# Operand sums of the second FFN product: on GpSimd, or in DRAM by copies and accumulating DMAs

## The chip, the core and the metric

The kernel runs on one core of a Trainium2 chip. The metric is the device time of one execution in microseconds (us). Matmuls run on TensorE (PE in the profile), the rest on VectorE (DVE), ScalarE (ACT) and GpSimd (POOL); SyncE (SP) issues most of the DMAs, POOL those that add to their destination.

## What is computed

One inference step of a two-layer encoder, for 1024 prompt rows and 64 sample rows (1088 in all) of width 1024, in float32. Layer 0 is a Mamba-2 mixer and a feed-forward block, layer 1 a band attention and a feed-forward block. The change concerns the feed-forward blocks:

```python
def swiglu(u, w_in, w_out):
    g, up = jnp.split(u @ w_in, 2, axis=-1)
    return (jax.nn.silu(g) * up) @ w_out

xp = xp + rmsnorm(swiglu(rmsnorm(xp, nw[2]), ffn_w_in[layer], ffn_w_out[layer]), nw[3])
```

`w_in` is 1024 x 5632, `w_out` 2816 x 1024. The output must agree with the float32 result, so each operand is split into a high and a low part and every product takes three matmuls.

## The kernel before, in words

**Layout.** Activations are kept transposed: features on the 128 partitions, rows of the batch on the free axis. The 1088 rows form four quarters of 256, 256, 288 and 288; half 0 (b = 0) is the two of 256, half 1 (b = 1) the two of 288.

**Two FFN products, both in a seven-product scheme.** Both large products are done by the Strassen-Winograd scheme: a matrix is cut into 2 x 2 quarters, and seven products of sums of quarters replace eight. The first FFN product (`run_pair`) does it for each pair of weight tiles: seven products P1 to P7 of 12 matmuls each, whose evictions by DVE, ACT and POOL give two hidden tiles. A few hidden tiles of half 0 are made by plain products (`plain_pairs`) instead. For the hidden matrix, the quarters are a11, a12, a21, a22: the row index is the quarter of the half, the column index the half of the 22 hidden tiles (`c, k = divmod(t_, K2)`, K2 = 11). The second FFN product needs, for each k of 0 to 10, the seven operands a11, a12, a22 and the sums s1, s2, s3, s4.

**Where the operands are kept.** `Hidden` keeps them in a DRAM scratch (`hscr`), one tensor for each layer and half, `[128, 7, 11 * n]` with n = 256 or 288; `OPS` gives the place of each operand. `Hidden.put` is called as each quarter of a (b, k) is done. It stores a11, a12 and a22 at once (SP, L1292) and keeps a21. When all four are there, POOL makes the sums in SBUF and each is stored by SP:

| line | sum | tile |
|---|---|---|
| L1307 | s3 = a11 - a21 | s3 |
| L1309 | s1 = a21 - a22 | in place of a21 |
| L1311 | s2 = s1 - a11 | in place of a11 |
| L1313 | s4 = a12 + s2 | in place of a12 |

The compiler moves instructions, so that L1307 (which needs only column 0) is seen after the first pair of a k, and the other three after the second.

**Order of the first product.** Six plain pairs of half 0 (k = 8 to 10, both columns), then 16 pairs of weights that serve both halves (k = 0 to 7; the middle), then six pairs for half 1 alone (k = 8 to 10; the tail). The weights of a pair come by two loads of 512 KB (SP, L253) into two raw buffers; POOL subtracts quarters (L291, L292), DVE adds (L309, L310), and ACT and DVE split the sums into high and low parts (L341, L342; for one quarter POOL does the low part, L342). The evictions are L1368 to L1388: L1371 is DVE's for P6, L1373 that for P2, and L1385 and L1388 are POOL's multiplications that end a hidden tile.

**Order of the second product.** `SEQ` lists the operands: a11, s2, s3, s1, a22, a12, s4, each for four output tiles p, 11 values of k and both halves (s4 one half after the other): 264 matmuls an operand. `loader` brings the operands from DRAM (SP, L1422) in this order, two values of k in a tile, and splits them (L1423, L1424). It takes an operand 9 us (`HD_W`) of planned time after its store. The products are added by DVE (ACT for the first) into the four quarters of the output (L1584 to L1597), which begin to leave in a22 and s4.

**Planned time.** The order of instructions is made by a planner (`Stream`): its clock `st.t` advances with the matmuls that are emitted (2360 columns a us), and side tasks are generators that run when their delay in it has passed. Matmuls keep their order as written; the other engines' instructions are ordered by priority and readiness when the program is built. Every engine takes its own queue in order, and so does SP with its DMAs: one that waits holds all behind it.

**The same kind of sum for the weights.** The sums of the second product's weights are made in DRAM already (`side_sums`, scratch `tscr`), during the mixers: copies by SP (L588), additions by accumulating DMAs from POOL (L591), each held until the newest matmul emitted at that point has run:

```python
def now(x):
    tc.add_manual_dep(x.ins, last[0].ins.name, AT, reason="its turn")
```

Of the kernel before, what the change touches and what calls it, by code (L numbers as in the profile page):

```python
# [16 lines left out]
P = 128  # L17
# [17 lines left out]
K2 = FT // 2  # L35
# [12 lines left out]
ES = 0.5, 0.5, 0.0  # L48
OS = 1.9, 1.4
EP_W, ER_W, EQ_W = (4.0, 7.0, 7.0, 5.0), (5.0, 8.9, 8.9, 7.0), 24.0  # L50
TS_W, HD_W, UT_W = 15.0, 9.0, 24.0

HIP = 3000
BYP = 0, 0, 800, 800
# [322 lines left out]
def hybrid_kernel(  # L377
# [197 lines left out]
    for b in range(2):  # L575
        for half in range(2):
            W.plan(*[dict(src=[w_so[m][:, half * 1024:(half + 1) * 1024]]) for mg in MGS for m in mg])

    def side_sums(layer):

        w2, td = w_f2[layer], td_[layer]
        KH = K2 * P

        def now(x):
            tc.add_manual_dep(x.ins, last[0].ins.name, AT, reason="its turn")

        def plain(p, i, src):
            now(nc.sync.dma_start(td[:, p, i], src))  # L588

        def more(p, i, src):  # L590
            now(G.dma_start(td[:, p, i], src, accum_op=ALU.add))  # L591
# [624 lines left out]
    def chain(layer, q, y, ss, cw, xsrc, xout, cpre, done):  # L1216
# [63 lines left out]
    class Hidden:  # L1280
# [9 lines left out]
        def write(self, op, b, k, x):  # L1290
            n = self.ops[b].n
            nc.sync.dma_start(self.hd[b][:, OPS[op], k * n:(k + 1) * n], x)  # L1292
            self.written[op, b, k] = st.t

        def put(self, t_, b, half, x):

            c, k = divmod(t_, K2)
            row = half ^ b
            got = self.got.setdefault((b, k), {})
            nm_ = f"a{row + 1}{c + 1}"  # L1300
            got[nm_] = x
            if nm_ != "a21":
                self.write(nm_, b, k, x)
            if len(got) == 4:
                g = G.tensor_tensor
                s3 = self.tmp.tile([P, 288], F32, tag=f"s3{b if k in BOTH else k % 2}", name="s3")[:, :self.ops[b].n]
                g(s3, got["a11"], got["a21"], op=ALU.subtract)  # L1307
                self.write("s3", b, k, s3)
                g(got["a21"], got["a21"], got["a22"], op=ALU.subtract)  # L1309
                self.write("s1", b, k, got["a21"])  # L1310
                g(got["a11"], got["a21"], got["a11"], op=ALU.subtract)  # L1311
                self.write("s2", b, k, got["a11"])
                g(got["a12"], got["a12"], got["a11"], op=ALU.add)  # L1313
                self.write("s4", b, k, got["a12"])

    def plain_pairs(ts, ops, hid, px):

        n = ops.n
        ws = [(W.get(), W.get()) for t_ in ts]
        for q in range(2):  # L1320
            st.wait_for(lambda: all(a_ in ops.plain for a_ in (f"a{q + 1}1", f"a{q + 1}2")))
            uq = ops.plain[f"a{q + 1}1"] + ops.plain[f"a{q + 1}2"]
            for t_, w2 in zip(ts, ws):
                x = hid.tile(t_, 0, q)

                def gate(ps):
                    with tc.high_priority(HIP):
                        A.activation(x, ps[:, :n], AF.Silu)

                def mult(ps):  # L1330
                    with tc.high_priority(HIP):
                        V.tensor_tensor(x, ps[:, :n], x, op=ALU.mult)
                    hid.put(t_, 0, q, x)

                for w, e in zip(w2, (gate, mult)):
                    unit(w, uq, n, e, pl=px)
                    if q:
                        W.put()

    def run_pair(t_, pr, bs, ends, ops, hid, px, tmp, apart=False):  # L1340


        tb = {b: {} for b in bs}
        for (p_, key, c0, i), b in [(x, b) for b in bs for x in PRODS] if apart else [(x, b) for x in PRODS for b in bs]:
            h, v = pr[key]
            n, x = ops[b].n, tb[b]

            def t_new(tag):
                return tmp.tile([P, n], F32, tag=f"{tag}{b if len(bs) > 1 else t_ // K2}", name=tag)

            st.wait_for(lambda: i in ops[b].hl)
            ah, al = ops[b].hl[i]
            ps = (px.tile([P, 512], F32, tag="mm", name="px") if p_ != P1 else mm("px"))[:, :n]
            for k in range(4):
                wh, wl = h[:, c0 + k * P:c0 + (k + 1) * P], v[:, c0 + k * P:c0 + (k + 1) * P]
                PE.matmul(ps, wh, ah[:, k, :], start=(k == 0), stop=False)  # L1356
                PE.matmul(ps, wh, al[:, k, :], start=False, stop=False)  # L1357
                last[0] = PE.matmul(ps, wl, ah[:, k, :], start=False, stop=(k == 3))  # L1358
                if k == 1:
                    st.run(6 * n / MMR)  # L1360
            st.t += 6 * n / MMR
            if b in ends:
                for r in ops[b].rings[i]:
                    r.put()
            with tc.high_priority(HIP):
                if p_ == P1:
                    x["p1"] = t_new("p1")
                    A.copy(x["p1"], ps)  # L1368
                elif p_ == P6:
                    x["u2"] = t_new("u2")  # L1370
                    V.tensor_tensor(x["u2"], ps, x["p1"], op=ALU.add)  # L1371
                elif p_ == P2:
                    V.tensor_tensor(x["p1"], ps, x["p1"], op=ALU.add)  # L1373
                    A.activation(x["p1"], x["p1"], AF.Silu)
                elif p_ == P7:
                    x["u3"] = hid.tile(t_, b, 1)
                    V.tensor_tensor(x["u3"], ps, x["u2"], op=ALU.add)
                elif p_ == P5:
                    x["c22"] = hid.tile(t_, b, 0)
                    V.tensor_tensor(x["c22"], ps, x["u3"], op=ALU.add)  # L1380
                    V.tensor_tensor(x["u2"], ps, x["u2"], op=ALU.add)
                elif p_ == P4:
                    V.tensor_tensor(x["u3"], ps, x["u3"], op=ALU.add)
                    A.activation(x["u3"], x["u3"], AF.Silu)
                    G.tensor_tensor(x["u3"], x["u3"], x["c22"], op=ALU.mult)  # L1385
                else:
                    V.tensor_tensor(x["u2"], ps, x["u2"], op=ALU.add)
                    G.tensor_tensor(x["c22"], x["p1"], x["u2"], op=ALU.mult)  # L1388
# [10 lines left out]
    def back(layer, start, cpost, xsrc, xmid, cpre, cpost2, xout, rb_out, done2):  # L1399

        dn, ops, phase, hid = [], [Ops(0, layer), Ops(1, layer)], [0], {}
        with ExitStack() as es:
# [152 lines left out]
            for op, bs in SEQ:  # L1555
# [3 lines left out]
                for p in range(4):  # L1559
# [17 lines left out]
                    for b in bs:  # L1577
# [3 lines left out]
                        c21, c22 = yq[q2][:, p, :], yq[q2][:, 4 + p, :]  # L1581
                        with tc.high_priority(HIP):
                            if op == "a11":
                                A.copy(c11, ps[b])  # L1584
                            elif op == "s2":
                                V.tensor_tensor(c12, ps[b], c11, op=ALU.add)
                            elif op == "a12":
                                V.tensor_tensor(c11, ps[b], c11, op=ALU.add)
                            elif op == "s3":
                                V.tensor_tensor(c21, ps[b], c12, op=ALU.add)  # L1590
                            elif op == "s1":
                                V.tensor_tensor(c22, ps[b], c21, op=ALU.subtract)
                                V.tensor_tensor(c12, ps[b], c12, op=ALU.subtract)
                            elif op == "a22":
                                V.tensor_tensor(c21, ps[b], c21, op=ALU.add)
# [537 lines left out]
```

## Time and profile before

| what | value |
|---|---|
| median of 3 runs (lowest, highest) | 3026.42 us (3023.85, 3032.41) |
| the profiled execution | 3029.47 us |
| its span, first to last instruction | 3027.8 us |
| mean granted TensorE clock | 0.985 of full |
| mean DMA rate | 131 GB/s |

The profile gives, for each engine, the time in which it executed something, for each group of instructions the count, the mean time and the idle time ahead of it with what ended it, and for each DMA the time from issue to landing. A DMA's issue has the line of its statement; waits of an issuing queue are marked SPq. Times in the views are counted from the start of the span. In a line of the timeline, the bracket has the idle time of the engine just before and who ended it. "issue" is time in which an engine waited for nothing that the profile shows.

### The profile page before, as it was taken

How to read it: one execution, taken by the hardware profiler on the slowest of the kernel's cores; microseconds unless marked ns; L12 is line 12 of the kernel's file. 1: busy time of each engine (PE TensorE's matmuls, PEld its weight loads, DVE VectorE, ACT ScalarE, POOL GpSimd, SP SyncE). 2: the span in 40 equal slices, each digit the busy share in tenths (PEclk: the TensorE clock that was granted, in tenths of full speed). 3: DMA queues.
4: the chain of work that ended last, by engine and by line, in shares of the span. 5: the costliest groups of instructions: out<-in, count | busy, mean ns of one | idle time of the engine just before them, and what ended most of it. 6: DMA issues, size and time to landing. Idle time of an engine off the chain costs nothing. (4 is left out here: it accounts for less than half of the span.)

```text
span 3027.8 us, 58411 instructions
## 1 busy us (share of the span) xinstructions
PE 2916.3 (96%) x22247; PEld 2850.9 (94%) x22247; DVE 2104.0 (69%) x4679; ACT 1447.8 (48%) x2677; POOL 903.7 (30%) x1081
## 2 busy tenths in 40 slices
PE   8999999999999999989998899999999999998998
PEld 7999999989999999989997899999899999998998
DVE  7778788885768554566569777777768754566457
ACT  6756565663453332234345556556554322333343
POOL 1333333340123545562023000000033555455011
PEclk9999999999999999999999999999999999999999
DMA  3023343345654223245565234444476232244565
GB/s 120 33 89 99 95 99 93 99 112 156 190 152 139 95 98 100 98 147 191 173 196 167 82 108 128 116 110 115 136 220 202 93 110 92 96 148 155 181 214 175
DMA packets 215273, 395.39 MB, mean 131 GB/s; under 512 B 21040, under 2 KB 138928, under 8 KB 214992
## 3 DMA queue, kind: packets, MB, share of 16 engines
q1 hardware_dynamic: 208592, 362.22, 36.6%
q0 software_dynamic: 6400, 29.43, 5.6%
q8 instruction: 175, 2.87, 0.4%
q14 instruction: 106, 0.87, 0.1%
HBM read 306.14 MB, written 127.12 MB: 143 GB/s over the span
## 5 line engine op out<-in xcount | busy, mean ns | idle before, releaser
L456 PE MATMUL mm<-r,hl 128*128 128x384 f32 (+2 forms) x1664 | 557.4, 335 | 7.2 <-DVE dt L738 3.4
L458 PE MATMUL mm<-r,hl 128*128 128x384 f32 (+2 forms) x1664 | 543.4, 327 | 4.9 <-DVE hl L355 4.2
L457 PE MATMUL mm<-r,hl 128*128 128x384 f32 (+2 forms) x1664 | 542.4, 326 | 0.0
L342 DVE TENSOR_TENSOR hl<-raw,hl 128x1024 fp32r<-128x1024 f32 (+2 forms) x219 | 250.4, 1144 | 155.3 <-ACT hl L341 154.6
L1357 PE MATMUL px<-r,hl 128*128 128x288 f32 (+1 forms) x1184 | 349.8, 295 | 0.0
L456 PEld LDWEIGHTS mm<-r,hl 128*128 128x128 f32 x1664 | 318.6, 191 | 9.6 <-ACT BT L815 3.7
L1356 PE MATMUL px<-r,hl 128*128 128x288 f32 x1056 | 314.2, 298 | 13.5 <-DVE u L1371 13.3
L458 PEld LDWEIGHTS mm<-r,hl 128*128 128x128 f32 x1664 | 318.0, 191 | 7.0 <-DVE hl L355 6.0
L457 PEld LDWEIGHTS mm<-r,hl 128*128 128x128 f32 x1664 | 318.7, 192 | 0.0
L1358 PE MATMUL px<-r,hl 128*128 128x288 f32 x1056 | 313.0, 296 | 0.0
L341 ACT CAST hl<-raw 128x1024 fp32r<-128x1024 f32 (+2 forms) x219 | 204.2, 938 | 201.1 <-PE po L1572 95.6
L482 POOL TENSOR_TENSOR ssum<-ssum,sq 128x256 f32<-128x256 f32 (+1 forms) x108 | 113.7, 1059 | 532.8 <-ACT sq L481 520.2
L1357 PEld LDWEIGHTS px<-r,hl 128*128 128x128 f32 x1184 | 224.8, 190 | 0.0
L1358 PE MATMUL px<-rx,hl 128*128 128x256 f32 x768 | 216.1, 281 | 6.7 <-DVE hl L342 6.7
L1356 PE MATMUL px<-rx,hl 128*128 128x256 f32 x768 | 216.5, 282 | 2.8 <-ACT hl L341 2.8
L1356 PEld LDWEIGHTS px<-r,hl 128*128 128x128 f32 x1056 | 200.6, 190 | 15.7 <-DVE u L1371 15.6
L1358 PEld LDWEIGHTS px<-r,hl 128*128 128x128 f32 x1056 | 200.4, 190 | 0.1
L1572 PE MATMUL po<-r,hl 128*128 128x288 f32 x616 | 182.8, 297 | 4.0 <-DVE hl L342 4.0
L1572 PE MATMUL po<-rx,hl 128*128 128x256 f32 x616 | 173.0, 281 | 12.7 <-DVE hl L342 12.7
L1570 PE MATMUL po<-r,hl 128*128 128x288 f32 x616 | 183.2, 297 | 0.0
L1571 PE MATMUL po<-r,hl 128*128 128x288 f32 x616 | 182.8, 297 | 0.0
L1357 PE MATMUL px<-rx,hl 128*128 128x256 f32 x640 | 179.7, 281 | 0.0
(365 smaller groups left out, 8547.3 us busy)
## 6 DMA issues: line engine op xcount, KB each, us to landing
raw<-in_w_f_dram SPq DMA_DIRECT2D x112, 512.0 KB, 3.4
tscr<-in_w_f_dram POOLq DMA_DIRECT2D x32, 704.0 KB, 7.0
raw<-in_w_in_dram SPq DMA_DIRECT2D x40, 512.0 KB, 3.4
r<-hscr SPq DMA_DIRECT2D x70, 288.0 KB, 4.8
hscr<-hid SPq DMA_DIRECT2D x132, 144.0 KB, 1.9
rx<-hscr SPq DMA_DIRECT2D x70, 256.0 KB, 3.7
hscr<-hid SPq DMA_DIRECT2D x132, 128.0 KB, 1.7
raw<-in_w_so_dram SPq DMA_DIRECT2D x32, 512.0 KB, 3.7
```

The source lines that it names most:

```text
L341: self.nc.scalar.copy(h, v)
L342: (eng or self.eng or self.nc.vector).tensor_tensor(lo, v, h, op=ALU.subtract)
L456: PE.matmul(ps[:, :n], h_, xh, start=(first and i == 0), stop=False)
L457: PE.matmul(ps[:, :n], h_, xl, start=False, stop=False)
L458: last[0] = PE.matmul(ps[:, :n], l_, xh, start=False, stop=(end and i == nk - 1))
L482: (eng or G).tensor_tensor(ssum[:, :n], ssum[:, :n], q[:, :n], op=ALU.add)
L1356: PE.matmul(ps, wh, ah[:, k, :], start=(k == 0), stop=False)
L1357: PE.matmul(ps, wh, al[:, k, :], start=False, stop=False)
L1358: last[0] = PE.matmul(ps, wl, ah[:, k, :], start=False, stop=(k == 3))
L1570: PE.matmul(ps[b], wh, xh, start=(k == 0), stop=False)
L1571: PE.matmul(ps[b], wh, xl, start=False, stop=False)
L1572: PE.matmul(ps[b], wl, xh, start=False, stop=(k == K2 - 1))
```

## The change

The operands of the second product are summed in DRAM.

- The quarters a11 and a22 (row and column equal) are kept with turned sign: in the plain pairs the multiplication, in the fast pairs the eviction ahead of it (P5's or P3's) is a scalar_tensor_tensor with the factor -1 in place of a tensor_tensor.
- `put` stores a11, a12 and a22 in their places and a21 by one DMA into both s3 and s1.
- When all quarters of a piece of k (0 to 3, 4 to 7, 8 to 10; `PCS`) are stored for a half, a task `sums` is spawned with a delay of `HD_W` = 9 us. It adds the turned a11 to s3 (which becomes a21 - a11) and the turned a22 to s1 by accumulating DMAs from POOL; 9 us (`SC_W`) later SP copies s1 to s2, 9 us later POOL adds the turned a11 to it, 9 us later SP copies s2 to s4, 9 us later POOL adds a12. Each is held by `now`, which moves out of `side_sums`.
- No POOL sums and no stores of sums are left.
- `OPS` is reordered (s3 beside s1), `SEQ` takes s3 ahead of s2, and the evictions of the second product follow the new order and signs: s2's product is added into two quarters, so there is one DVE instruction more for each p and half.

```diff
-TS_W, HD_W, UT_W = 15.0, 9.0, 24.0
+TS_W, HD_W, UT_W, SC_W = 15.0, 9.0, 24.0, 9.0
...
-    OPS = dict(a11=0, s2=1, a12=2, s3=3, s1=4, a22=5, s4=6)
+    OPS = dict(a11=0, a22=1, a12=2, s3=3, s1=4, s2=5, s4=6)
+    PCS = (range(0, 4), range(4, 8), range(8, 11))
 
     SEQ = (
-        ("a11", (0, 1)), ("s2", (0, 1)), ("s3", (0, 1)), ("s1", (0, 1)), ("a22", (0, 1)), ("a12", (0, 1)),
+        ("a11", (0, 1)), ("s3", (0, 1)), ("s2", (0, 1)), ("s1", (0, 1)), ("a22", (0, 1)), ("a12", (0, 1)),
...
         def put(self, t_, b, half, x):
 
             c, k = divmod(t_, K2)
-            row = half ^ b
-            got = self.got.setdefault((b, k), {})
-            nm_ = f"a{row + 1}{c + 1}"
-            got[nm_] = x
-            if nm_ != "a21":
-                self.write(nm_, b, k, x)
-            if len(got) == 4:
-                g = G.tensor_tensor
-                s3 = self.tmp.tile([P, 288], F32, tag=f"s3{b if k in BOTH else k % 2}", name="s3")[:, :self.ops[b].n]
-                g(s3, got["a11"], got["a21"], op=ALU.subtract)
-                self.write("s3", b, k, s3)
...
+            n = self.ops[b].n
+            nm_ = f"a{(half ^ b) + 1}{c + 1}"
+            cols = slice(k * n, (k + 1) * n)
+            if nm_ == "a21":
+                nc.sync.dma_start(self.hd[b][:, OPS["s3"]:OPS["s1"] + 1, cols], x.unsqueeze(1).to_broadcast([P, 2, n]))
+            else:
+                nc.sync.dma_start(self.hd[b][:, OPS[nm_], cols], x)
+                self.written[nm_, b, k] = st.t
+            got = self.got.setdefault((b, [k in r for r in PCS].index(True)), [])
+            got.append(k)
+            if len(got) == 4 * len(set(got)) and len(set(got)) == len(PCS[[k in r for r in PCS].index(True)]):
+                st.spawn(self.sums(b, min(got), max(got) + 1), HD_W)
+
+        def sums(self, b, k0, k1):
+
+            n, hd = self.ops[b].n, self.hd[b]
+            cols = slice(k0 * n, k1 * n)
+
+            def more(op, x):
+                now(G.dma_start(hd[:, OPS[op], cols], hd[:, OPS[x], cols], accum_op=ALU.add))
+                for k in range(k0, k1):
+                    self.written[op, b, k] = st.t
+
+            def copy(op, x):
+                now(nc.sync.dma_start(hd[:, OPS[op], cols], hd[:, OPS[x], cols]))
+
+            yield 0, 0
+            more("s3", "a11")
+            more("s1", "a22")
+            for op, x, y in (("s2", "s1", "a11"), ("s4", "s2", "a12")):
+                yield 0, SC_W
+                copy(op, x)
+                yield 0, SC_W
+                more(op, y)
...
-                        V.tensor_tensor(x, ps[:, :n], x, op=ALU.mult)
+                        if q == t_ // K2:
+                            V.scalar_tensor_tensor(x, ps[:, :n], -1.0, x, op0=ALU.mult, op1=ALU.mult)
+                        else:
+                            V.tensor_tensor(x, ps[:, :n], x, op=ALU.mult)
...
                     x["c22"] = hid.tile(t_, b, 0)
-                    V.tensor_tensor(x["c22"], ps, x["u3"], op=ALU.add)
+                    if 1 ^ b == t_ // K2:
+                        V.scalar_tensor_tensor(x["c22"], ps, -1.0, x["u3"], op0=ALU.mult, op1=ALU.subtract)
+                    else:
+                        V.tensor_tensor(x["c22"], ps, x["u3"], op=ALU.add)
...
-                    V.tensor_tensor(x["u2"], ps, x["u2"], op=ALU.add)
+                    if b == t_ // K2:
+                        V.scalar_tensor_tensor(x["u2"], ps, -1.0, x["u2"], op0=ALU.mult, op1=ALU.subtract)
+                    else:
+                        V.tensor_tensor(x["u2"], ps, x["u2"], op=ALU.add)
...
                             if op == "a11":
-                                A.copy(c11, ps[b])
+                                A.activation(c11, ps[b], AF.Copy, scale=-1.0)
+                            elif op == "s3":
+                                V.tensor_tensor(c21, c11, ps[b], op=ALU.subtract)
                             elif op == "s2":
                                 V.tensor_tensor(c12, ps[b], c11, op=ALU.add)
+                                V.tensor_tensor(c21, ps[b], c21, op=ALU.add)
```

More of the change, by code (lines that the diff above doesn't have):

```diff
@@ L577, in hybrid_kernel, with now @@
             W.plan(*[dict(src=[w_so[m][:, half * 1024:(half + 1) * 1024]]) for mg in MGS for m in mg])
+    def now(x):
+        tc.add_manual_dep(x.ins, last[0].ins.name, AT, reason="its turn")
     def side_sums(layer):
@@ L582, in side_sums @@
         KH = K2 * P
-        def now(x):
-            tc.add_manual_dep(x.ins, last[0].ins.name, AT, reason="its turn")
         def plain(p, i, src):
@@ L1288, in tile @@
             return self.tmp.tile([P, 288], F32, tag=f"{('c22', 'u3')[half]}{i}{t_ // K2}", name="hid")[:, :self.ops[b].n]
[L1290 to L1293, printed above, removed]
         def put(self, t_, b, half, x):
             c, k = divmod(t_, K2)
-            row = half ^ b
-            got = self.got.setdefault((b, k), {})
-            nm_ = f"a{row + 1}{c + 1}"
-            got[nm_] = x
-            if nm_ != "a21":
-                self.write(nm_, b, k, x)
-            if len(got) == 4:
-                g = G.tensor_tensor
-                s3 = self.tmp.tile([P, 288], F32, tag=f"s3{b if k in BOTH else k % 2}", name="s3")[:, :self.ops[b].n]
-                g(s3, got["a11"], got["a21"], op=ALU.subtract)
-                self.write("s3", b, k, s3)
[L1309 to L1314, printed above, removed]
@@ L1594, in back @@
                             elif op == "a22":
-                                V.tensor_tensor(c21, ps[b], c21, op=ALU.add)
+                                V.tensor_tensor(c21, c21, ps[b], op=ALU.subtract)
                             else:
```

2 lines of the change are left out of this document (removed).

## The prediction

> **What bounds the kernel now.** I read the page first, then the table of stages, then the chain of waits inside the stage that the change touches.
>
> ```profile
> span 3027.8 us, 58411 instructions
> PE 2916.3 (96%) x22247; PEld 2850.9 (94%) x22247; DVE 2104.0 (69%) x4679; ACT 1447.8 (48%) x2677; POOL 903.7 (30%) x1081
> ```
>
> TensorE is busy for 2916.3 of 3027.8 us, and the change leaves every matmul in place. So it can win at most what TensorE loses today near the code that it touches, and it loses whenever it makes TensorE wait. POOL's 30% says nothing by itself; what counts is whether a POOL instruction ends a wait of TensorE. I therefore looked for places where matmuls are missing. The table of stages gives, for five stretches, the matmuls done (x behind PE busy) and the granted clock (the third figure from the end).
>
> ```profile
> 1100.00:1300.00 200.00, 199.94 (x1604) 199.74 (x1604) 103.75 (x184) 61.44 (x103) 101.98 (x101) 1.00 0.33 109
> 1316.00:1387.00 71.00, 62.30 (x424) 61.04 (x425) 47.56 (x63) 25.11 (x39) 44.50 (x33) 0.93 0.42 135
> 2701.00:2783.00 82.00, 68.31 (x475) 66.92 (x473) 58.71 (x78) 33.13 (x51) 51.44 (x40) 0.93 0.44 144
> 940.00:975.00 35.00, 29.46 (x230) 28.86 (x229) 32.22 (x34) 14.28 (x18) 17.85 (x12) 0.90 0.34 109
> 2340.00:2368.00 28.00, 23.21 (x183) 22.81 (x182) 25.22 (x25) 11.53 (x15) 17.95 (x10) 0.94 0.32 105
> ```
>
> The first stretch is the middle of the first FFN product of layer 0, where every weight pair serves both token halves: TensorE never stops, and 200.00 us / 1604 = 0.1247 us for one matmul of 272 columns on average (256 and 288 take turns), so 0.132 us for one of 288. The next two are its tails in layers 0 and 1, in which six weight pairs serve only half 1 (288 columns). There 424 matmuls should take 56.0 us and took 71.0; 475 should take 62.7 and took 82.0. The last two are its heads, where the plain pairs give way to the first fast pair: at 0.1247 they should take 28.7 and 22.8 us and took 35.0 and 28.0. So a tail loses 15.0 us in layer 0 and 19.3 in layer 1, part of it at a granted clock of 0.93 after each stop, and a head loses 6.3 and 5.2. Of the 19.3, 4.2 are this row, the first matmul of the second product, which waits for the load of an operand that the change doesn't touch:
>
> ```profile
> PE po L1572 <- DVE hl L342: 4.2, 1, 4.2
> ```
>
> What stops TensorE in a tail is seen in the chain of waits of layer 1 (start, us, what):
>
> ```profile
> 2725.35 0.62 POOL tt L291
> ...
> 2726.62 0.83 POOL hid L1385
> 2727.45 1.67 POOL half L342
> 2729.12 1.69 POOL tt L292
> 2730.81 1.74 POOL hid L1388
> 2732.63 1.66 POOL hid L1309
> 2734.37 0.82 POOL hid L1311
> 2735.25 1.69 POOL hid L1313
> 2736.95 0.32 SPq L1292
> 2737.37 3.69 DMA raw<-in_w_f_dram
> 2741.19 1.33 POOL tt L291
> 2742.55 1.29 DVE tt L309
> 2743.89 1.52 issue
> 2745.41 0.46 DVE u L1371
> 2745.91 0.40 PE px L1356
> ```
>
> Read from the bottom: TensorE waits for DVE's eviction L1371, which stands in DVE's queue behind the weight sum L309, which waits for POOL's L291, which waits for the weights. Their load starts only at 2737.37, because SP takes its queue in order and the store ahead of it (L1292) waits for L1313. L1309, L1311 and L1313 are sums that the change removes, with L1307. The waits carry it: the largest of TensorE between 2695 and 2780 us is
>
> ```profile
> PE px L1356 <- DVE u L1371: 6.4, 3, 2.9
> ```
>
> **What the change removes.** Each of 11 hidden rows k, 2 halves and 2 layers loses four POOL sums (176 instructions). In a tail they come in turns: one after the first pair of a k (L1307), three after the second.
>
> ```profile
> 2718.51 1.67 POOL L1307 TENSOR_TENSOR s<-hid 128x288 f32<-128x288 f32 x1
> 953.38 4.20 POOL L1307 TENSOR_TENSOR s<-hid 128x256 f32<-128x256 f32 x1 [9.54 <-DVE hid L1332]
> 957.54 1.32 POOL L291 TENSOR_TENSOR tt<-raw 128x512 f32<-128x512 f32 x1
> ```
>
> In the chain the three sums lie between the end of L1388 and SP's store: from 2732.63 to 2736.95, 4.3 us. One L1307 is 1.67. L291 recurred after 15.8 us (2725.35 to 2741.19); 15.8 - 4.3 = 11.5, where TensorE needs 84 x 0.132 = 11.1 for a pair. After the edit the store after L1388 is the last thing ahead of the load, so what is late next is that load's own 3.69 us, and 0.4 us of each pair stay. Tail: 13 of the 15 us come back, **-13** in each layer (bounds -15, all of it, and -5, if the load is then held by its buffer and only L1307 counts, 3 x 1.67).
>
> In the head L1307 took 4.20 us and L291 followed at once. L291 could start as soon as its weights have landed, which the rows don't date, so between 0 and 4.2 us: **-3**, nearer to the upper end since L291 had no wait of its own left.
>
> **What it adds.** Each piece (rows 0 to 3, 4 to 7, 8 to 10) of each half gets four accumulating DMAs issued by POOL and two copies issued by SP, and the store of a21 becomes one of double size. A piece of four rows is 512 KB (half 0) or 576 KB (half 1). The nearest rows are those of the weight sums of the same form:
>
> ```profile
> q1 hardware_dynamic: 208592, 362.22, 36.6%
> q0 software_dynamic: 6400, 29.43, 5.6%
> tscr<-in_w_f_dram POOLq DMA_DIRECT2D x32, 704.0 KB, 7.0
> tscr<-tscr SPq DMA_DIRECT2D x16, 704.0 KB, 4.3
> hl<-in_w_f_dram POOLq DMA_DIRECT2D x7, 512.0 KB, 10.6
> L591 POOL DMA_DIRECT2D tscr<-in_w_f_dram x32 | 26.6, 831 | 225.5 <-PE mm L458 213.2 <-PE mmx L458 6.5 <-DVE zs L768 5.6
> SPq L588 <- PE mm L458: 78.3, 16, 13.0
> ```
>
> q0 spent 5.6% of 3027.8 = 170 us of all 16 engines on 29.43 MB, 5.76 us a MB: 3.0 us for 512 KB and 3.4 for 576 KB. The 704 KB (0.72 MB) is 4.15 by that and landed after 7.0, so 2.9 us are delay. q1 has 1108 us for 362.22 MB, 3.06 us a MB: a copy is 1.8 us. Both halves end a piece together, so four accumulating DMAs queue up: 2 x 3.0 + 2 x 3.4 + 2.9 = 15.7 us until s1 of half 1 has landed. The generator lets SP take the copy 9 us (SC_W) after those were issued. It waits for that landing, and SP takes nothing behind it: the stores L1292, the next weight loads L253, in the second product the operand loads L1422. So SP stands 15.7 - 9 = 6.7 us, once per piece. The second round has two accumulating DMAs, 3.0 + 3.4 + 2.9 = 9.3 us against 9, and holds nothing. On POOL each issue is 0.83 us (L591), against 0.8 to 1.7 for each sum removed; behind one that waits for its copy stand L291, L1385 and L1388 of the next pair; the copy is issued 9 us earlier and lands in 4.3, so an accumulating DMA of the second round waits only where SP's hold passed 4.7 us, by 2 us.
>
> Where does a hold of 6.7 us show? In the middle of the first product there is room:
>
> ```profile
> 1194.18 1.31 POOL L291 TENSOR_TENSOR tt<-raw 128x512 f32<-128x512 f32 x1 [6.18 <-DVE hid L1380]
> 1203.75 0.42 DVE L1371 TENSOR_TENSOR u<-px,p 128x256 f32<-128x256 f32 x1 [2.95 <-PE px L1358]
> ```
>
> From L291 to L1371 were 9.6 us here and 4.2 in the chain above (2741.19 to 2745.41), where nothing was spare: 5.4 us of cover. The loads there also come after the sums that go, some 4 us earlier, so 9.4 us cover 6.7 and the cost is nothing; without the cover it would be 6.7 and a stretch at half clock. In the tail the second piece ends just as the six pairs begin, and pairs then follow at 11.5 against 11.1: no cover but a start some 2 to 4 us earlier. I put it at **+7** in each layer: 6.7, less 2, and some 2 for the clock that falls after a stop (the stretches above were granted 0.93; bounds 0 if SP's copy falls behind the loads, +12 if the accumulating DMAs share the engines with the loads and land at 20 us).
>
> At the start of the second product the third piece follows with three rows; s3 is needed some 30 us later (the first operand is 264 matmuls at 0.1247 = 33 us) and s2 another 33 later, against 9 + 15.7 and 18 + 15.7 + 9.3 us: covered by the first operand. For SP's hold against the weights there, **+1** (0 to +4). The eight additional DVE evictions of that product in a layer and the turned sign cost TensorE nothing:
>
> ```profile
> L1586 DVE TENSOR_TENSOR yq<-po,yq x16: 418/437/458, 1436.5 to 2847.1; 128x256 f32<-128x256 f32 x8, 128x288 f32<-128x288 f32 x8
> L1477 DVE SCALAR_TENSOR_TENSOR yq<-yq,pcs,rb x56: 471/493/2657, 1577.0 to 3009.8; 128x256 f32<-128x256 f32 x32, 128x288 f32<-128x288 f32 x24
> ```
>
> Eight of 0.44 us lie beside 33 us of matmuls. The turned sign makes an eviction a scalar_tensor_tensor, whose nearest row (L1477, from SBUF) has a median of 493 ns against 437: 0.06 more in an eviction, hidden in the middle, where DVE is busy for 103.75 of 200 us.
>
> Sum: -13 - 3 + 7 + 1 = -8 in a layer, -16 in all. The profiled execution took 3029.47 us, 1.7 beyond its span and 3.05 above the median of 3026.42; -16 from the median is **3010**.
>
> **The Trainium skill on one price.** The trace has 7.0 us for an accumulating 704 KB. "DMA: Bandwidth & Descriptors" (the Trainium skill), section "Anatomy of one DMA — SWDGE (gpsimd) path", fits about 2 us plus the bytes at 436 GB/s, an estimate of 3.7 us here; by it the four would land in 7.4 us, SP would not stand at all, and the sum would be -15 a layer, 2996. The trace says otherwise, and I stay with it.
>
> **The rivals.** *No change that can be measured* (0.3%, 9 us, is about what can be told): the sums go, but the load's buffer or DVE's queue ends the wait next. For it: TensorE's waits there go through DVE's queue, and DVE stays 67% busy in the tail (47.56 of 71). Against it: the chain shows L253 issued 0.42 us after the store, as soon as SP was free. With -5 and 0 for the two gains and +3 for the hold, -2 a layer: 3022.
>
> *Slower*: the hold on SP. Its place is the first copies of pieces one and two, its price the landing of four accumulating DMAs. If these take 10.6 us, as the row in the busy stage did for 512 KB, and only half of it overlaps, the last lands at 10.6 + 3 x 5.3 = 26 us; SP stands 17 us where 9.4 are covered in the middle and 2 in the tail: 8 + 15, with 2 each for the clock 27, against the 13 + 3 won: +11 a layer, 3048. L588 speaks for it: such copies held SP for 78.3 / 16 = 4.9 us even where the source had landed. Against: the tail's DMA share is 0.42, the 7.0 row is of the same kind and larger. It decides from a landing of some 22 us on: then 13 us of standing cost 4 + 11 + 4 = 19, more than is won.
> "SBUF — State Buffer" (the Trainium skill), section "SBUF: two separate sides", says that GpSimd can't write a DMA's descriptors while certain DVE instructions hold a port that both share; that would push the landing to this side where DVE is busy, and the 10.6 against 7.0 agrees with it but has a DMA-heavy stage as another reason.
>
> **How the numbers follow.** Forecast (3010, its own range 2992 to 3017): 0.56. No change (3017 to 3035): 0.16. Slower: 0.28. These are the chances of faster, same and slower. The range runs from 2992 (-17 a layer, no hold) to 3045, which leaves out the far half of the slower case and a little below.
>
> **What would show it.** Right: in the tails L291 recurs every 11 to 12 us; TensorE's waits for L1371 there fall from 6.4 to about 3, now behind SP's copy; POOL loses some 180 us (176 sums of about 1 us); q0 grows by 24.5 MB (11 rows x 272 KB x 4 sums x 2 layers). Wrong: SP's copies hold over 13 us, weight loads right behind them, and new stops of TensorE in the stretch 1100 to 1300.

## The result: 0.3% slower, where 0.5% faster was forecast

The changed kernel takes 3036.77 us (median of 8 runs) against 3026.9 for the kernel before; the ratio of the means is 1.0029, with a 95% interval of 1.0016 to 1.0042. The forecast of 3010 had the wrong sign; 3036.77 lies inside the range up to 3045. Its profiled execution took 3034.74 us (span 3033.0); from its page:

```profile
PE 2911.3 (96%) x22247; PEld 2841.7 (94%) x22247; DVE 2085.6 (69%) x4695; ACT 1443.9 (48%) x2677; POOL 773.1 (25%) x953
q0 software_dynamic: 13312, 53.95, 10.2%
```

POOL is busy for 131 us less (773.1 against 903.7), and q0 has grown by the 24.5 MB that were forecast. So the change did what it says. To see where time came and went, the stages are counted again, now so that they cover both first FFN products and the starts of the second ones. A row of these tables has the stretch, its length, TensorE's busy time with the number of matmuls, the granted clock, the DMA engines' busy share and GB/s. In each layer: head, the second half of the middle, tail, start of the second product. The counts are of one profiled execution of each kernel. First the kernel before:

```profile
935.00:980.00 45.00, 39.46 (x316) 0.92 0.31 97
1160.00:1300.00 140.00, 139.94 (x1123) 1.00 0.33 112
1300.00:1390.00 90.00, 79.16 (x554) 0.94 0.43 138
1390.00:1450.00 60.00, 56.08 (x431) 0.94 0.56 184
2335.00:2375.00 40.00, 35.21 (x278) 0.96 0.27 87
2560.00:2700.00 140.00, 139.96 (x1118) 1.00 0.34 114
2700.00:2785.00 85.00, 71.17 (x490) 0.92 0.44 144
2785.00:2830.00 45.00, 45.00 (x350) 0.96 0.61 198
```

Then the changed kernel:

```profile
935.00:980.00 45.00, 40.85 (x339) 1.00 0.41 111
1160.00:1300.00 140.00, 137.55 (x1088) 1.00 0.43 130
1300.00:1390.00 90.00, 77.35 (x546) 0.94 0.71 203
1390.00:1450.00 60.00, 56.11 (x438) 0.97 0.72 208
2335.00:2375.00 40.00, 36.98 (x290) 0.96 0.43 120
2560.00:2700.00 140.00, 137.36 (x1092) 1.00 0.37 116
2700.00:2785.00 85.00, 71.65 (x498) 0.94 0.74 206
2785.00:2830.00 45.00, 38.57 (x292) 0.92 0.83 246
```

At 0.1247 us a matmul, the heads gain 23 and 12 matmuls (2.9 and 1.5 us). The middles, which did not stop before, lose 35 and 26 (4.4 and 3.2 us). The tails, where 13 us should have come back, stand where they stood (-8 and +8). The start of the second product of layer 1 loses 58 (7.2 us). The column ahead of the last says what is new: in the tails and the starts of the second product the DMA engines are busy for 0.71 to 0.83 of the time instead of 0.43 to 0.61.

What a stop looks like is seen in the tail of layer 0. The timeline of SP, POOL and DVE (start, us, what; in brackets the idle time just before and who ended it):

```profile
1318.54 1.41 SPq L1444 DMA_DIRECT2D rx<-hscr  x3
...
1322.82 3.91 SPq L253 DMA_DIRECT2D raw<-in_w_f_dram  x2
1326.83 0.48 SPq L1318 DMA_DIRECT2D hscr<-hscr  x1
...
1319.80 1.65 POOL L1313 DMA_DIRECT2D hscr<-hscr  x2
1337.08 1.30 POOL L291 TENSOR_TENSOR tt<-raw 128x512 f32<-128x512 f32 x1 [5.71 <-DMA raw<-in_w_f_dram]
...
1338.41 1.27 DVE L309 TENSOR_TENSOR tt<-tt,raw 128x512 f32<-128x512 f32 x1 [7.35 <-POOL tt L291]
1341.27 0.45 DVE L1387 TENSOR_TENSOR u<-px,p 128x288 f32<-128x288 f32 x1
```

L253 is the weight load, L1444 an operand load of the second product (L1422 before), L1313 an accumulating DMA, L1318 a copy, L1387 the eviction that was L1371. SP issued both weight loads (at 1322.82 and 1326.39) **before** its copy at 1326.83; no copy held them. POOL's L291 nevertheless waited 5.71 us for the data and ran at 1337.08, so DVE's L309 and, behind it, L1387 came late, and TensorE stopped. The loads were on their way all that time, beside two accumulating DMAs issued at 1319.80.

Another wait for an accumulating DMA did stand ahead of these loads: the operand load L1444 held SP for 6.9 us, until 1318.54. What it cost can be worked out against experiment 1 below, which has no DMA sums. There the two loads went out 5.5 and 7.8 us after the L291 of the pair before; here (L291 at 1316.06) after 6.8 and 10.3. L291 needs the second. It ran 4.1 us after that load's issue there, and 10.7 us after it here. Of the 9.2 us by which L291 came late, 2.6 are a late issue and 6.6 a late landing.

The DMA view of the tail (1316 to 1387; first the busy tenths in 40 slices, then issues with their median from issue to landing) of the changed kernel:

```profile
DMA  9999999999992204999910207999700289999999
raw<-in_w_f_dram SPq DMA_DIRECT2D x6, 512.0 KB, 7.2
hscr<-hscr POOLq DMA_DIRECT2D x4, 576.0 KB, 8.9
```

In the first twelve slices, 21 us, the engines are busy for 90% or more. The same weight loads land after 7.2 us; in the kernel before they took 3.6 in this window:

```profile
raw<-in_w_f_dram SPq DMA_DIRECT2D x8, 512.0 KB, 3.6
```

The waits over the whole run (who waited for whom: us in total, times, the longest): TensorE still waits for L1387, up to 6.1 us at a time. SP waits for accumulating DMAs with its copies and with its operand loads:

```profile
PE px L1372 <- DVE u L1387: 19.4, 13, 6.1
SPq L1318 <- DMA hscr<-hscr: 30.0, 8, 6.2
SPq L1444 <- DMA hscr<-hscr: 19.5, 4, 7.4
```

The 6.2 us of the copies look like the forecast hold of 6.7, but they aren't where it was forecast. The copies' longest waits are 5.3 and 6.2 us at the starts of the second product and 2.9 and 5.2 in the middles. In the tails (1300 to 1390, 2700 to 2785) no copy waited for a DMA; there an operand load did, once in each (6.9 and 7.4 us).

### The profile page after: what moved, and what is told of

Read it like the earlier page. It is cut to its first block, busy times and chain, and to the rows that moved or that the text cites. A ratio compares the mean times of both kernels' runs of the same rounds, so it can differ in the third digit from the quotient of the medians.

```text
span 3033.0 us, 58051 instructions
## 1 busy us (share of the span) xinstructions
PE 2911.3 (96%) x22247; PEld 2841.7 (94%) x22247; DVE 2085.6 (69%) x4695; ACT 1443.9 (48%) x2677; POOL 773.1 (25%) x953
## 3 DMA queue, kind: packets, MB, share of 16 engines
q0 software_dynamic: 13312, 53.95, 10.2%
## 4 chain that ended last, share of the span: by engine, by line
PE 45%; DVE 8%; DMA 7%; issue 3%; ACT 3%; POOL 2%; SPq 0%; POOLq 0%; DVEq 0%; ACTq 0%
PE px L1372 6%; PE px L1373 6%; PE px L1374 6%; PE po L1594 4%; PE po L1592 4%; PE po L1593 4%; DMA raw<-in_w_f_dram 4%; PE mm L456 2%; PE mm L458 2%; PE mm L457 2%; PE mmx L456 1%; PE po L1909 1%; PE mmx L458 1%; PE mmx L457 1%; DVE hl L342 1%
## 5 line engine op out<-in xcount | busy, mean ns | idle before, releaser
L1372 PE MATMUL px<-rx,hl 128*128 128x256 f32 x768 | 216.3, 282 | 4.7 <-DVE hid L1402 2.7
L1374 PE MATMUL px<-rx,hl 128*128 128x256 f32 x768 | 214.9, 280 | 4.9 <-DVE hl L342 4.9
L1594 PE MATMUL po<-rx,hl 128*128 128x256 f32 x616 | 173.4, 281 | 9.3 <-DVE hl L342 9.3
L1592 PE MATMUL po<-rx,hl 128*128 128x256 f32 x616 | 173.4, 282 | 6.9 <-ACT hl L341 6.9
```

The source lines that it names most:

```text
L1592: PE.matmul(ps[b], wh, xh, start=(k == 0), stop=False)
L1594: PE.matmul(ps[b], wl, xh, start=False, stop=(k == K2 - 1))
```

## The experiments

Three theories were to be told apart. **A**: the accumulating DMAs keep the DMA engines busy, and the weight loads and operand loads beside them land late. **B**: SP is held by its copies, which wait for the accumulating DMAs (the prediction's own term). **C**: issuing the added DMAs costs, by their number. A further question was whether the gain forecast from taking the sums off POOL exists at all. "Before" and "after" mean the two kernels of this document.

**1. The sums simply left out.** Edit to after: no accumulating DMAs, no copies.

```diff
-                now(G.dma_start(hd[:, OPS[op], cols], hd[:, OPS[x], cols], accum_op=ALU.add))
...
-                now(nc.sync.dma_start(hd[:, OPS[op], cols], hd[:, OPS[x], cols]))
+                pass
...
-    OPS = dict(a11=0, a22=1, a12=2, s3=3, s1=4, s2=5, s4=6)
+    OPS = dict(a11=0, a22=1, a12=2, s3=3, s1=4, s2=3, s4=4)
```

> The changed kernel without the accumulating DMAs and without the copies: the sums are left out (s2 and s4 are loaded from the places of s3 and s1), loads, matmuls and evictions stay. What is left is the removal of the POOL sums alone. Every theory: the gains seen in the trace of the changed kernel stay and the losses go, so heads, tails and the step to the second product give 15 to 20 us a layer: 2987 to 3000 us. Above 3015 the loss would lie in the new order of operands or in the evictions, not in the DMAs.

Measured: 2995.89 us, ratio to before 0.9889 (0.9875 to 0.9904). The gain is there: 1.11% of 3027, 34 us. So neither the new order of operands nor the changed evictions carry the loss. Its stages:

```profile
935.00:980.00 45.00, 40.98 (x343) 1.00 0.31 97
1160.00:1300.00 140.00, 139.74 (x1121) 1.00 0.32 105
1300.00:1390.00 90.00, 84.21 (x622) 0.98 0.48 158
1390.00:1450.00 60.00, 60.00 (x488) 1.00 0.58 183
2335.00:2375.00 40.00, 39.13 (x298) 0.96 0.25 80
2560.00:2700.00 140.00, 139.99 (x1106) 1.00 0.35 114
2700.00:2785.00 85.00, 79.59 (x595) 0.96 0.52 171
2785.00:2830.00 45.00, 45.00 (x367) 1.00 0.56 174
```

Against before, the heads gain 27 and 20 matmuls, 3.4 and 2.5 us. Tail and start together gain 68 + 57 = 125 in layer 0 and 105 + 17 - 12 = 110 in layer 1 (the 12 because the tail begins earlier there), 15.6 and 13.7 us. Against this run, the changed kernel then lacks 4 + 33 + 76 + 50 = 163 matmuls in layer 0 and 8 + 14 + 97 + 75 = 194 in layer 1: 20 and 24 us. By the ratios the added DMAs cost 1.0029 - 0.9889 = 1.40%, 42 us. The DMA view of its tail:

```profile
DMA  0204890020784020389002078225999999804548
raw<-in_w_f_dram SPq DMA_DIRECT2D x6, 512.0 KB, 3.6
```

**2. The copies issued by POOL.** This empties SP's queue of the waits that B blames.

```diff
-                now(nc.sync.dma_start(hd[:, OPS[op], cols], hd[:, OPS[x], cols]))
+                now(G.dma_start(hd[:, OPS[op], cols], hd[:, OPS[x], cols]))
```

> The changed kernel with its copies issued by POOL instead of SP, so that SP never waits for an accumulating DMA; the bytes are the same. Theory A (the accumulating DMAs and copies share the 16 engines with the weight loads, which land late: 7.2 us instead of 3.6 in the tail): nothing much changes, 3028 to 3042. Theory B (SP's queue is held by the copies, as predicted): the holds go, 3000 to 3015.

Measured: 3043.17 us, ratio 1.0044 (1.0028 to 1.006), 1 us above what A gave it. Over the whole run nothing is won. By stages two things happened. The second halves of the middles hardly stop any more, 33 and 21 matmuls better than after (4.1 and 2.6 us):

```profile
1160.00:1300.00 140.00, 140.00 (x1121) 1.00 0.42 126
2560.00:2700.00 140.00, 139.56 (x1113) 1.00 0.40 120
```

The tails do 505 and 456 matmuls, 41 and 42 fewer than after, and in that of layer 0 the weight loads still land late:

```profile
raw<-in_w_f_dram SPq DMA_DIRECT2D x6, 512.0 KB, 8.1
```

So the loss in the middle hangs on the copies in SP's queue, together with late loads. In two pairs of layer 0 the second load took 8.0 to 8.8 us to L291 in both kernels, but with the copies in SP's queue it went out 14.1 us after the L291 before, without them 11.9 and 12.9, and TensorE went on. In the tails B falls, since no copy waited for a DMA there in after. So it isn't the main cause. The copies' waits are not gone: they stand in POOL's queue now (44.0 us in 6 waits, 9.4 at the longest), with L291 and the multiplications L1404 and L1410 behind them, and this run doesn't say how much of the tails' further loss they cause. "DMA: Bandwidth & Descriptors" (the Trainium skill), section "Issuing engines are not separate DMA queues", says that DMAs from any engine run on the same 16 engines and interleave, so that another issuer saves issue time only. The run agrees in its sum: another issuer, 1.0044.

**3. The copies alone.** Edit to after: the accumulating DMA is taken out, the copies by SP stay.

```diff
             def more(op, x):
-                now(G.dma_start(hd[:, OPS[op], cols], hd[:, OPS[x], cols], accum_op=ALU.add))
```

> The changed kernel without the accumulating DMAs; the copies stay on SP, each still held until its matmul has run (s2 and s4 are plain copies of a21). Theory A (shared engines): most of the traffic is gone, so nearly the time without any, at most 6 us above it: 2990 to 3005. Theory B (SP held): the landings that SP waits for are gone, but its waits for the matmul stay; a middle value, 3005 to 3025.

Measured: 2997.98 us, ratio 0.9892 (0.9875 to 0.9908), which can't be told from experiment 1. The copies cost nothing that was measured when there is no accumulating DMA to wait for; in the tail the weight loads take 3.7 us. All but some 1 us of the 42 belongs to the accumulating DMAs, or to what the copies do in their presence.

**4. The kernel before, its sums 3 us later.** An attempt to keep the sums on POOL and let the weight load pass them in SP's queue.

```diff
-                g = G.tensor_tensor
...
+                s = self.sums(b, k, got)
+                if (b, k) == (1, K2 - 1):
+                    next(s)
+                else:
+                    st.spawn(s, SD_W)
```

with `SD_W` = 3.0 and the four sums and stores moved unchanged into `sums`.

> The kernel before with its POOL sums kept, but made by a task 3 us of planned time later (the last k at once), so that a pair's weight loads go ahead of the sums' stores in SP's queue. If the stops in the tails come from SP's loads standing behind the stores of sums, most of them go without any DMA in their place: 3000 to 3015. If POOL's own time ahead of the weight sums is what counts, little changes: 3020 to 3028.

Measured: 3027.08 us, ratio 0.9989 (0.9979 to 0.9998). A miss, and it decides nothing: the edit didn't reach the queue. SP's queue in the tail still has the stores, four of them with their wait, ahead of the load:

```profile
1341.94 4.72 SPq L1292 DMA_DIRECT2D hscr<-hid  x4
1346.75 0.38 SPq L253 DMA_DIRECT2D raw<-in_w_f_dram  x1
```

The other engines' instructions are ordered by readiness when the program is built, and a later call alone doesn't move them.

**5. Only rows 8 to 10 in DRAM.** The rows of the middle, 0 to 7, are summed by POOL again, where POOL has time; so a third of the accumulating DMAs is left.

```diff
-    PCS = (range(0, 4), range(4, 8), range(8, 11))
+    PCS = (range(8, 11),)
...
+            if not any(k in r for r in PCS):
+                got = self.got.setdefault((b, k, "pool"), {})
...
+                    g(s3, got["a21"], got["a11"], op=ALU.add)
```

> The changed kernel, but rows 0 to 7 are summed by POOL and stored as before; only rows 8 to 10 (the heads and tails, where POOL's sums ended waits of TensorE) are summed by DMAs, in one piece for each half. Theory A (shared engines): the head's DMAs fall in the middle, which has cover; the tail has no accumulating DMA of its own rows until it ends; what remains is the start of the second product, 2 to 9 us a layer. Gains of 4 (head) and 8 to 10 (tail, whose start still has the POOL sums of row 7): 3005 to 3018, below the kernel before. If the mere presence of accumulating DMAs costs what they cost in the change: 3025 to 3035.

Measured: 3017.03 us, ratio 0.9961 (0.9946 to 0.9976): 0.68% better than after. In the tail's window the weight loads land after 3.6 us again, and its L291 starts at 1324.12, 1335.68 and 1347.03, as often as forecast. What is lost moved to where the remaining piece runs. That of half 0 falls into the first half of the middle:

```profile
980.00:1160.00 180.00, 177.84 (x1421) 1.00 0.35 107
```

Before and after did 1442 and 1445 there, without a stop. In layer 1 (2375 to 2560) it does 1444, where they did 1486 and 1481.

**6. One row in a piece.** Same bytes, 128 or 144 KB in a DMA, four times as many issues or nearly: 176 accumulating DMAs in place of 48.

```diff
-    PCS = (range(0, 4), range(4, 8), range(8, 11))
+    PCS = tuple(range(k, k + 1) for k in range(11))
```

> The changed kernel with pieces of one row instead of three or four: the same bytes in 176 accumulating DMAs and 88 copies instead of 48 and 24, spread over the first product. Theory A (a weight load lands late when a long accumulating DMA shares the engines with it): each now takes a quarter of the engines' time, so the middle loses nothing and the tail less: 3005 to 3022. Theory C (each issue on POOL, 0.83 us, or the number of DMAs is what counts): 3040 and above.

Measured: 3022.92 us, ratio 0.9982 (0.9972 to 0.9991), 1 us above what A gave it. More DMAs cost less, so C falls as the main cause. The weight loads of the tail:

```profile
raw<-in_w_f_dram SPq DMA_DIRECT2D x7, 512.0 KB, 4.2
```

q0 is busy for more time than in after (11.9% against 10.2%), and yet the kernel is faster by 0.47%. So the total time on the engines doesn't set the cost. What fits is that it counts how much stands in a weight load's way at once, but the run doesn't show that alone: SP's waits changed with the pieces too, and the middle, where A expected no loss, did 1096 and 1106 matmuls, 27 and 12 fewer than before.

**7. Plain DMAs in place of the adding ones.** Same bytes, same issuer, the same dependences in the program; the addition is left out.

```diff
-                now(G.dma_start(hd[:, OPS[op], cols], hd[:, OPS[x], cols], accum_op=ALU.add))
+                now(G.dma_start(hd[:, OPS[op], cols], hd[:, OPS[x], cols]))
```

> The changed kernel with plain copies of the same bytes in place of the accumulating DMAs, still issued by POOL (the additions are left out). By q1's 3.06 us a MB against q0's 5.76 they hold the engines about half as long. Theory A: about half of the 40 us that the accumulating DMAs cost comes back: 3010 to 3025. If the issue on POOL and its waits are the cost, nothing comes back: 3035 to 3042.

Measured: 3007.66 us, ratio 0.9927 (0.9912 to 0.9941), 2 us below A's range and far from C's. Of the 42 us over experiment 1, 0.38% or 12 us are left. Against experiment 1, q0 over the whole run and the tail's weight loads:

```profile
q0 software_dynamic: 12288, 53.95, 8.0%
raw<-in_w_f_dram SPq DMA_DIRECT2D x6, 512.0 KB, 5.9
```

The added 24.5 MB take 8.0% of 3006.8 less 5.7% of 2997.5 (experiment 1's q0), 70 us of all engines, or 2.8 us a MB; in after it is 10.2% of 3033.0 less the same 171, 138 us or 5.6 a MB. Half the time on the engines, and a good quarter of the cost. This supports A, but since the DMAs also land earlier it doesn't part A from B everywhere: SP's copies waited for 16.0 us instead of 30.0, and the second halves of the middles did 1120 and 1104 matmuls. In the tail of layer 0 the lateness can be read as above: the second load of the same pair was issued at 1320.52 and L291 ran at 1326.85, 6.3 us later, between the 4.1 of experiment 1 and the 10.7 of after.

**8. Rows 8 to 10 in one-row pieces.** Experiments 5 and 6 together.

```diff
-    PCS = (range(0, 4), range(4, 8), range(8, 11))
+    PCS = (range(8, 9), range(9, 10), range(10, 11))
```

> As the kernel with only rows 8 to 10 summed by DMAs, but in pieces of one row, so that rows 8 and 9 of half 1 are summed during the tail and only row 10 in the second product. Theory A: short DMAs cost the tail a little (loads late by a microsecond or so each) and spare the start of the second product: 3002 to 3015, within 8 us of the kernel with one piece. If any accumulating DMA in the tail costs a stop as in the change: 3020 to 3030.

Measured: 3020.8 us, ratio 0.9968 (0.9956 to 0.998), not better than experiment 5; a miss by 6 us, inside the range given to the other case (any accumulating DMA in the tail costs a stop). By stages, the first half of the middle does 1437 and 1471 matmuls against 1421 and 1444 in experiment 5, but the tails 562 and 529 against 593 and 553: here rows 8 and 9 of half 1 are summed during the tail, where experiment 5 has almost no accumulating DMA. So shorter pieces help in the middle, and sums that now fall into the tail, where nothing is spare, cost there.

**9. The sums on POOL, held for 6 us.** Back to before, with no added DMA. If the gain comes from the order alone (sums behind the next weight load), no DMA is needed for it. The sums of rows 7 to 9 of half 1 are made by a task 6 us later, and the first two are held by `now` so that they can't be moved ahead.

```diff
+                if b and K2 - 1 > k >= K2 - NB0 // 2 - 1:
+                    st.spawn(self.sums(b, k, got, now), SD_W)
+                else:
+                    next(self.sums(b, k, got, lambda x: x))
...
+            hold(g(s3, got["a11"], got["a21"], op=ALU.subtract))
...
+            hold(g(got["a21"], got["a21"], got["a22"], op=ALU.subtract))
```

with `SD_W` = 6.0.

> The kernel before, all sums on POOL, no DMAs added; the sums of rows 7, 8 and 9 of half 1 are made 6 us of planned time later and are held until the newest matmul at that point has run, so that in the tail a pair's weight loads go out first and POOL adds while they are under way. If the stops of the tail come from the loads that stand behind POOL's sums, this recovers much of what leaving out the sums' DMAs did there, 8 to 12 of 13 us a layer: 3003 to 3014. If POOL's total of work in the tail is the limit, it stays at 3020 to 3030.

Measured: 3010.85 us, ratio 0.9938 (0.9923 to 0.9952). This beats both kernels. SP and POOL in the tail of layer 0:

```profile
1337.76 0.33 SPq L253 DMA_DIRECT2D raw<-in_w_f_dram  x1
...
1339.45 1.79 POOL L1314 TENSOR_TENSOR s<-hid 128x288 f32<-128x288 f32 x1
...
1344.72 1.32 POOL L291 TENSOR_TENSOR tt<-raw 128x512 f32<-128x512 f32 x1
```

The weight loads are issued at 1337.76 and 1339.94, ahead of the stores; the sums run from 1339.45 on while the loads are under way, and L291 follows at 1344.72, 12.5 us after the one before it. The three rows of layer 1, from the second half of the middle to the start of the second product:

```profile
2560.00:2700.00 140.00, 136.65 (x1066) 0.98 0.38 125
2700.00:2785.00 85.00, 79.70 (x599) 0.98 0.48 161
2785.00:2830.00 45.00, 45.00 (x367) 1.00 0.66 208
```

The tail's 599 alone would mislead: a stop that falls just behind 2700 in before falls just ahead of it here, and is counted in the row above. Together the three do 2032 matmuls, against 1958 before and 2068 without any sums, so 74 of 110 are back. In layer 0 it is 77 of 123 (2185, against 2108 and 2231). These 151 matmuls are 18.8 us, the measured gain.

**10. The same with 9 us.**

> The same with 9 us. By the first theory the same within 5 us, 3003 to 3018, unless the sums then meet the next pair's weight sums (L291) and hold them up, 3015 to 3025; by the second 3020 to 3030.

Measured: 3022.78 us, ratio 0.9978 (0.997 to 0.9987). Two thirds of the gain are gone. SP and POOL in the tail of layer 0:

```profile
1323.94 7.52 SPq L1292 DMA_DIRECT2D hscr<-hid  x4
1332.40 2.21 SPq L253 DMA_DIRECT2D raw<-in_w_f_dram  x2
...
1338.57 1.30 POOL L291 TENSOR_TENSOR tt<-raw 128x512 f32<-128x512 f32 x1 [6.19 <-DMA raw<-in_w_f_dram]
```

At 9 us the sums reach so far into the next pair that their stores stand ahead of the following load again: SP is busy with four of them until 1331.46, and only then come the loads, for which L291 waits.

## Why the prediction was wrong, point by point

**What bounds the kernel, and the gain: right.** TensorE stopped in the tails because the sums on POOL stood, through SP's store, ahead of the weight load. Without them and with nothing in their place, a head gained 3.4 and 2.5 us (forecast 3), a tail with the start of the second product 15.6 and 13.7 (forecast 13), and L291 in the tail started at 1315.78, 1327.64, 1338.81 and 1350.69, 11.2 to 11.9 us apart (forecast 11.5). Experiment 9 shows the cause from the other side: the same sums on the same engine, only later, bring 19 us. One row was misread without effect on a term: the wait of 4.2 us (L1572) isn't the first matmul of the second product, which began at 2774.14; it ends at 2783.13.

**What costs nothing: right.** The turned sign has no price; DVE's scalar_tensor_tensor from PSUM takes a mean of 438 ns (L1397, 38 times), where the tensor_tensor row of the prediction had a median of 437.

**What is added: the step that failed.** The prediction had +7 in the tail, 0 in the middle and +1 at the start, 8 a layer or 16 in all. Measured are 42 us (1.40%). By matmuls against experiment 1 the second half of the middle cost 4.1 us in layer 0 and 1.7 in layer 1 (33 and 14 matmuls), tail and start together 15.7 and 21.4 (126 and 172).
- In the tail the mechanism was another one. The +7 was a hold of SP by its first copy, 6.7 us; in neither tail did a copy wait for a DMA, and the weight loads of the stop at 1337 had been issued ahead of the copy. An operand load did hold SP there, which the sum didn't have, but at that stop late issue made 2.6 us and late landing 6.6.
- The prediction did price the engines' time well: 5.76 us a MB against 5.6. It then used it only to date the landing of the accumulating DMAs themselves. That the same engines carry the weight loads, and that a load among them would land at 7.2 instead of 3.6 us in a tail without slack, was not in any term. It was named only as an upper bound of the tail term, and there as a cause for a later landing of the accumulating DMAs, not of the weights.
- In the middle the predicted mechanism is part of it: copies in SP's queue and late loads together stopped TensorE, and with the copies on POOL it went on (experiment 2). The cover of 9.4 us was compared with SP's hold alone, while the load itself, 3.69 us in the prediction's chain, took over 8.
- The start of the second product, with its loads of operands and weights together, was taken as covered because the *sums* had 30 us to spare. The loads had not (those of 256 KB operands landed there after 6.7 and 6.9 us, in experiment 1 after 3.8 and 4.0), and it is here that SP's copies waited longest (5.3 and 6.2 us), where the sum had +1.

**The rivals.** "Slower" had the right sign by the wrong mechanism: its place (SP's copies ahead of the loads of middle and tail) was met in the middle only, and copies that wait 6.2 us at most are far from its 17 us of standing; the slowest group of accumulating DMAs had a median of 10.5 us. "No change" went by the load's buffer or DVE's queue taking back most of the gain; experiment 1 shows the gain whole. The Trainium skill's fit named in the prediction ("DMA: Bandwidth & Descriptors", section "Anatomy of one DMA — SWDGE (gpsimd) path") gives an estimate of 2 us and 0.59 MB at 436 GB/s, 3.4 us for those 576 KB; the measured 10.5 speaks against it for DMAs that add, in this traffic. The 7.4 us that the prediction has for the four by this fit are 7.1 if their 2.23 MB are taken at once, also an estimate; SP wouldn't stand by either.

**The signs.** In the tail of layer 0, L291 recurred after 21.0, 15.3 and 14.1 us, not after 11 to 12. POOL fell by 131 us of busy time, not 180: its instructions fell by 128 (1081 to 953), which is the 176 sums less 48 accumulating DMAs that count as POOL's own; at about 0.83 us an issue these make up 40 of the missing 49. q0 grew as forecast. TensorE's wait for the eviction did not fall to 3 but rose from 6.9 to 10.5 in the tail of layer 0 and stayed at 6.4 in that of layer 1. Of the signs that were named against the forecast, new stops between 1100 and 1300 appeared; holds of over 13 us did not.

**Open.** Whether a weight load is late because packets queue at the 16 engines or because of the memory behind them, no run separates; the full slices of the DMA view and experiment 7 fit the engines. How the 42 us divide between late loads and SP's waits is known only at the places worked out above: no run takes away all of SP's waits (copies and operand loads) and leaves the accumulating DMAs. The port that the prediction names as a possible reason for late landings was not tested.

## What to carry to other kernels

Price a DMA twice: once for who waits for it, and once for what else is on the engines while it runs. A load that is just in time pays for a neighbour that nobody waits for. Where work on an engine stands ahead of a load only by its place in a queue, move it behind the load first; here that took no new DMA and gave 0.6% with the right delay (6 us; at 9 us most of it was lost again), while moving the work to the DMA engines lost 0.3%.

## What was not expected of the hardware

- An accumulating DMA from DRAM to DRAM occupies the engines about twice as long as a plain one of the same bytes from the same issuer (5.6 against 2.8 us a MB, all 16 engines together). The kernel lost more than in proportion: 42 us against 12, the waits for their landing included.
- 512 KB weight loads beside such DMAs landed after 7.2 us instead of 3.6; beside plain ones after 5.9, beside one-row accumulating ones after 4.2, though these kept the engines busy for longer in all.
